# A rotation kernel whose first and last 16 images are cut into four pieces, in 8-row runs

## Chip, cores, metric

One core of one Trainium2 chip. The metric is the device time of one execution in microseconds (us), which in these runs is about 1.8 us more than the span of the profile. All runs compared here are at a granted clock of 1.0. "Tile" below means 16 images (4.2 MB in, 4.2 MB out); there are six, numbered 0 to 5. DVE is the Vector engine; SP and ACT are the engines whose queues issue the loads and the outputs.

## The reference

```python
batch, c, h, w = 32, 3, 256, 256
x = np.random.randn(batch, c, h, w).astype(np.float32)
return np.rot90(x, k=1, axes=(-2, -1)).astype(np.float32)
```

96 images of 256x256 float32 are rotated by 90 degrees: 25.17 MB are read and 25.17 MB written, and nothing is computed.

## The kernel before

A partition holds a run of R = 16 rows of an image, and 32 partitions hold the runs of two images. DVE transposes 32x32 blocks with strided access patterns, so that a partition ends up with 16 rows of the rotated image.

```python
R = 16; K = H // R; A = 32 // K; G = 4 * A * A; F = R * W   # K 16, A 2, G 16, F 4096
x_v = x.rearrange("b c h w -> (b c h w)").rearrange(
    "(g b a qk f) -> g b qk a f", b=A, a=A, qk=4 * K, f=F)
o_v = ...                                                   # [cut: the same for the output, with a and b exchanged]
in_pool = ...tile_pool(name="in_pool", bufs=3)
out_pool = ...tile_pool(name="out_pool", bufs=3)
for g in range(N // G):
    S = in_pool.tile([P, A, F], fp32, name="S")
    for b in range(A):
        nc.sync.dma_start(out=S[:, b], in_=x_v[g, b])       # 2 MB, in 16 KB packets
    U = out_pool.tile([P, A, F], fp32, name="U")
    ...                                                     # [cut: the views src and dst]
    for q in range(R):
        nc.vector.transpose(dst[:, q], src[:, q])           # 16 of 128x512
    for a in range(A):
        nc.scalar.dma_start(out=o_v[g, a], in_=U[:, a])     # 2 MB, in 16 KB packets
```

## Time and profile before

| | before |
|---|---|
| time, median (range) | 124.6 us (124.37 to 124.67) |
| span of the profile | 122.7 us |
| DVE busy | 90.7 us (74%) |
| first DMA packet starts, last one ends | 2.13 us, 121.59 us |
| 16 KB packets per DMA engine, usual duration | 192, 611 ns: 117.3 us |

The first three rows are from the page and the times; the last two are counted from the packet records of the trace. From the page, with the span in 40 slices of 3.07 us (busy tenths for DVE and DMA, then the rate), then the costliest group and the DMA issues:

```profile
span 122.7 us, 182 instructions
DVE 90.7 (74%) x96; POOL 0.2 (0%) x4
...
DVE  0000699999999999999999999999906999930000
...
DMA  3999999999999999999999999999999999999992
GB/s 85 406 433 443 427 427 427 427 427 427 310 432 432 433 433 427 427 433 432 419 433 438 427 427 427 432 438 432 432 427 438 438 427 433 433 427 427 427 432 101
...
L49 DVE STREAM_TRANSPOSE U<-S 128x512 f32<-128x512 f32 x96 | 90.7, 1055 | 17.7 <-DMA S<-in_x_dram 13.3
...
S<-in_x_dram SPq DMA_DIRECT2D x12, 2048.0 KB, 22.3
out_dram<-U ACTq DMA_DIRECT2D x12, 2048.0 KB, 23.3
```

Only one row is full from end to end: DMA. One slice, 31 to 34 us, falls to 310 GB/s; call it the dip. DVE is idle for four slices at the start and four at the end, but DMA is full in nearly all of them.

What DVE waits for (total us, times, longest; a wait of 0.2 us for itself is left out):

```profile
DVE U L49 <- DMA S<-in_x_dram: 13.3, 1, 13.3
DVE U L49 <- DMA out_dram<-U: 4.1, 1, 4.1
```

And the timeline (start us, duration us, engine, line) of the first issue, and of the last tile's transposes:

```profile
0.73 0.60 SPq L43 DMA_DIRECT2D S<-in_x_dram  x1
...
93.14 15.20 DVE L49 STREAM_TRANSPOSE U<-S 128x512 f32<-128x512 f32 x16 [4.15 <-DMA out_dram<-U]
```

The last tile's transposes end at 108.3 us. They are 15.2 us for 16, so 0.95 us from start to start, 1.86 ns per element. The Trainium skill ("Vector Engine (DVE) Microarchitecture Reference", "5.2 Measured stream behaviour on trn2") gives 1.71 to 1.98 ns per column for two-source streams that hop 4 KiB at every element of the output or of all operands, against 1.05 for contiguous ones. The transposes here read and write with strides at every element and lie within that. But they have one source and other steps, and that table has no row for a transpose, so this is a comparison and not an explanation.

### The profile page before, as it was taken

What the parts mean: (1) busy time and instruction counts of PE and PEld (TensorE: products, weight loads), DVE (VectorE), ACT (ScalarE), POOL (GpSimd) and SP (SyncE); (2) the same over time, 40 slices, a digit from 0 to 9 for tenths busy, and PEclk for the clock granted to TensorE, in tenths of its full rate; (3) what the DMA queues carried; (4) which work ended last, traced back from release to release, by engine and by line L of the source; (5) the groups of instructions that cost most, each with busy time, mean ns of one, the idle gap of its engine ahead of it and who ended that gap; (6) DMA issues with size and microseconds to landing.
All of it is one profiled execution on the core that took longest, in us unless ns stands there. A gap on an engine that the chain in (4) does not pass through costs nothing.

```text
span 122.7 us, 182 instructions
## 1 busy us (share of the span) xinstructions
DVE 90.7 (74%) x96; POOL 0.2 (0%) x4
## 2 busy tenths in 40 slices
DVE  0000699999999999999999999999906999930000
POOL 0000000000000000000000000000000000000000
DMA  3999999999999999999999999999999999999992
GB/s 85 406 433 443 427 427 427 427 427 427 310 432 432 433 433 427 427 433 432 419 433 438 427 427 427 432 438 432 432 427 438 438 427 433 433 427 427 427 432 101
DMA packets 3457, 50.34 MB, mean 410 GB/s; under 512 B 384, under 2 KB 384, under 8 KB 384
## 3 DMA queue, kind: packets, MB, share of 16 engines
q1 hardware_dynamic: 1728, 25.17, 48.9%
q10 hardware_dynamic: 1728, 25.17, 47.9%
q14 instruction: 1, 0.01, 0.0%
HBM read 25.17 MB, written 25.17 MB: 410 GB/s over the span
## 4 chain that ended last, share of the span: by engine, by line
DMA 53%; DVE 31%; SPq 1%; issue 1%; DVEq 1%; ACTq 0%
DVE U L49 31%; DMA out_dram<-U 28%; DMA S<-in_x_dram 26%; SPq L43 1%; DVEq L77 1%; ACTq L51 0%; DVEq L49 0%
## 5 line engine op out<-in xcount | busy, mean ns | idle before, releaser
L49 DVE STREAM_TRANSPOSE U<-S 128x512 f32<-128x512 f32 x96 | 90.7, 1055 | 17.7 <-DMA S<-in_x_dram 13.3
L66 POOL MEMSET const-uint8-127<- 128x1 uint8 x1 | 0.1, 102 | 0.0
L66 POOL MEMSET const-bfloat16-1.0<- 128x1 bf16 x1 | 0.1, 101 | 0.0
L66 POOL MEMSET const-float32-0.0<- 128x1 f32 x1 | 0.1, 98 | 0.2 <-issue 0.2
L66 POOL MEMSET const-float32-1.0<- 128x1 f32 x1 | 0.1, 98 | 0.0
## 6 DMA issues: line engine op xcount, KB each, us to landing
S<-in_x_dram SPq DMA_DIRECT2D x12, 2048.0 KB, 22.3
out_dram<-U ACTq DMA_DIRECT2D x12, 2048.0 KB, 23.3
```

Of the source, the lines that this page charges most:

```text
L43: nc.sync.dma_start(out=S[:, b], in_=x_v[g, b])
L49: nc.vector.transpose(dst[:, q], src[:, q])
L66: nc = _bacc.Bacc("TRN2", target_bir_lowering=False, num_devices=1)
L77: with _tile.TileContext(nc) as tc:
```

## The change

The two visible faults of the profile are the 13.3 us before DVE starts and the long end after DVE stops. The change cuts the first and the last tile into four pieces of 4 images: each is loaded, transposed (one 128x2048 instruction with 8-row runs) and put out on its own, so work should start after a quarter of a tile and the last output should be small. The middle four tiles stay as they were. In `KINDS`, 1 is a tile in pieces and 2 is a tile as before.

```diff
+    G = 16
+    KINDS = [1, 2, 2, 2, 2, 1]
+    for g, kind in enumerate(KINDS):
+        S = in_pool.tile([P, F], fp32, name="S")
+        U = out_pool.tile([P, F], fp32, name="U")
+        if kind == 1:
+            R = 8
+            ...                       [cut: views Sv, Uv, xv, ov in 4 contiguous pieces]
+            for s in range(4):
+                nc.sync.dma_start(out=Sv[:, s], in_=xv[s])        # 1 MB, 8 KB packets
+            for s in range(4):
+                src = Sv[:, s].rearrange("p (r k q) -> p q r k", r=R, q=R)[:, ::-1, :, ::-1]
+                dst = Uv[:, s].rearrange("p (q k r) -> p q r k", q=R, r=R)
+                nc.vector.transpose(dst, src)                     # one of 128x2048
+                nc.scalar.dma_start(out=ov[s], in_=Uv[:, s])
+        else:
+            ...                       [cut: R = 16, as before]
```

More of the change, by code (lines that the diff above doesn't have):

```diff
@@ L20 @@
     P = 128
-    R = 16
-    K = H // R
-    A = 32 // K
-    G = 4 * A * A
-    F = R * W
-    fp32 = mybir.dt.float32
-    x_v = x.rearrange("b c h w -> (b c h w)").rearrange(
-        "(g b a qk f) -> g b qk a f", b=A, a=A, qk=4 * K, f=F
-    )
-    o_v = out.rearrange("b c h w -> (b c h w)").rearrange(
-        "(g b a qk f) -> g a qk b f", b=A, a=A, qk=4 * K, f=F
-    )
+    G = 16
+    KINDS = [1, 2, 2, 2, 2, 1]
+    assert len(KINDS) * G == N
+    F = G * H * W // P
+    fp32 = mybir.dt.float32
@@ L37 @@
+    xf = x.rearrange("b c h w -> (b c h w)").rearrange("(g f) -> g f", g=N // G)
+    of = out.rearrange("b c h w -> (b c h w)").rearrange("(g f) -> g f", g=N // G)
     in_pool = ctx.enter_context(tc.tile_pool(name="in_pool", bufs=3))
     out_pool = ctx.enter_context(tc.tile_pool(name="out_pool", bufs=3))
-    for g in range(N // G):
-        S = in_pool.tile([P, A, F], fp32, name="S")
-        for b in range(A):
-            nc.sync.dma_start(out=S[:, b], in_=x_v[g, b])
-        U = out_pool.tile([P, A, F], fp32, name="U")
-        src = S.rearrange("p b (r k q) -> p q r k b", r=R, q=R)[:, ::-1, :, ::-1]
-        dst = U.rearrange("p a (q k r) -> p q r k a", q=R, r=R)
-        for q in range(R):
-            nc.vector.transpose(dst[:, q], src[:, q])
-        for a in range(A):
-            nc.scalar.dma_start(out=o_v[g, a], in_=U[:, a])
+    for g, kind in enumerate(KINDS):
[3 more added lines that the diff above has]
+            R = 8
+            Sv = S.rearrange("p (s f) -> p s f", s=4)
+            Uv = U.rearrange("p (s f) -> p s f", s=4)
+            xv = xf[g].rearrange("(s p f) -> s p f", s=4, p=P)
+            ov = of[g].rearrange("(s p f) -> s p f", s=4, p=P)
+            for s in range(4):
[6 more added lines that the diff above has]
+        else:
+            R = 16
+            Sv = S.rearrange("p (b f) -> p b f", b=2)
+            Uv = U.rearrange("p (a f) -> p a f", a=2)
+            xv = xf[g].rearrange("(b a qk f) -> b qk a f", b=2, a=2, f=F // 2)
+            ov = of[g].rearrange("(b a qk f) -> a qk b f", b=2, a=2, f=F // 2)
+            for b in range(2):
+                nc.sync.dma_start(out=Sv[:, b], in_=xv[b])
+            src = Sv.rearrange("p b (r k q) -> p q r k b", r=R, q=R)[:, ::-1, :, ::-1]
+            dst = Uv.rearrange("p a (q k r) -> p q r k a", q=R, r=R)
+            for q in range(R):
+                nc.vector.transpose(dst[:, q], src[:, q])
+            for a in range(2):
+                nc.scalar.dma_start(out=ov[a], in_=Uv[:, a])
```

## The prediction

> **What bounds it now.** The DMA engines. The page's slices show DMA at 9 or more tenths from about 3 to 120 us of the 122.7 us span, at 427 to 433 GB/s; the Vector engine (DVE) is busy 90.7 us (74%). The packet records of the trace give 611 ns for nearly every 16 KB packet. Moving 2 x 25.17 MB takes each of 16 engines 192 packets, 117.3 us. First packet at 2.13 us, last ends at 121.6 us. Outside the floor are: 2.1 us before the first packet, about 0.4 us of slow first packets, a dip at 31 to 34 us (310 GB/s in that slice, when the outputs' queue starts; about 0.9 us lost), 0.9 us of engines finishing unevenly, 1.1 us of end. The Trainium skill ("DMA: Bandwidth & Descriptors", "Where 436 GB/s comes from") states a ceiling of 435 GB/s; this trace's 429 is 99% of it.
>
> The 13.3 us that the DVE waits at the start cost nothing: input streams at full rate. At the other end the waits view shows the last tile's transposes starting at 93.1 us, after 4.1 us of waiting for tile 2's output, and ending at 108.3 us while a backlog of outputs keeps the DMA full.
>
> **What the change does.**
> - Bytes: unchanged. A third (4 pieces x 2 tiles x 2 directions, 1 MB each) go in 8 KB packets, 128 per engine. Half of 611 ns is 305.5; the one 8 KB packet that ran under load (an instruction fetch) took 309 ns. Cost 128 x 3.5 ns = +0.45 us, an estimate. The same page's "Why small descriptors are slow (HBM only)" gives about 3 cycles per packet, which agrees.
> - DVE: 32 transposes of 128x512 (0.95 us start to start) become 8 of 128x2048. At the same 1.85 ns per element each takes 3.8 us (I allow 2.2 to 4.5), 30 us for 30 us. DVE stays near 90 us.
> - First transpose near 5.7 to 6 us in place of 13.3, first output issued near 10 us in place of 28.6. But these outputs take turns with inputs on a full DMA. Gain on the critical path: none, except that the dip may go or move (0 to -0.9 us).
> - The end: the DMA is full until the end in both; smaller last outputs gain nothing.
> - New semaphore waits for issues: one input of tile 2 waits for the first output, two pieces of the last tile for outputs of tiles 1 and 2. Working out the schedule with packets taking turns, I get no idle DMA for 8-row transposes of up to about 6 us. Beyond 7 us each the last tile becomes DVE-bound (+6 us).
>
> **Prediction.** 124.6 + 0.45 (packets) - 0.5 (half the dip, a guess) = 124.5 us, range 123.3 to 126.0. Faster by over 2%: 3%; within 2%: 93%; slower by over 2%: 4%.
>
> **What would show it right.** DMA slices at 9 from 3 us to the end; 425 to 433 GB/s; first DVE start at 5.5 to 6.5 us with no gain in span; DVE busy 85 to 97 us, a 128x2048 at 3.3 to 4.3 us; a chain made mostly of DMA.
>
> **What would make it wrong.** 8 KB packets clearly slower than 309 ns (each 10 ns more is +1.3 us); 128x2048 transposes above 6 us; slices with DMA under 9 in the middle because a wait for an output holds up inputs; a mix of reads and writes from 10 us on that runs below 427 GB/s, which before's mixed stretch (33 to 93 us) does not show.

## The result, and the profile after

| | before | after |
|---|---|---|
| time, median (range) | 124.56 us (124.37 to 124.67), 4 runs | 124.09 us (124.01 to 124.19), 4 runs |
| ratio | | 0.9965, 95% interval 0.9947 to 0.9982 |
| span | 122.7 us | 122.2 us |
| DVE busy | 90.7 us | 91.3 us |
| first DVE start | 13.33 us | 5.67 us |
| first output issued | 28.58 us | 9.67 us |
| last load's last packet ends | 91.8 us | 105.8 us |
| last transpose ends | 108.3 us | 110.8 us |

A ratio in this document is the mean time of one kernel's fast runs over that of the other's in the same rounds, so it is not quite the ratio of the medians. The time fell by 0.35%, clear of noise and far under 2%. From the page of the changed kernel:

```profile
span 122.2 us, 170 instructions
DVE 91.3 (75%) x72; POOL 0.2 (0%) x4
...
DVE  0199999007999999999999990799999999092000
...
DMA  3999999999999999999999999999999999999993
GB/s 86 424 421 416 375 432 429 426 410 442 418 440 437 437 434 418 429 434 429 429 429 429 434 429 421 453 410 413 464 413 429 445 416 426 442 429 408 429 429 161
...
L65 DVE STREAM_TRANSPOSE U<-S 128x512 f32<-128x512 f32 x64 | 60.5, 1059 | 10.8 <-DMA S<-in_x_dram 7.1
L49 DVE STREAM_TRANSPOSE U<-S 128x2048 f32<-128x2048 f32 x8 | 31.0, 3937 | 8.7 <-DMA S<-in_x_dram 8.7
...
S<-in_x_dram SPq DMA_DIRECT2D x8, 2048.0 KB, 21.1
out_dram<-U ACTq DMA_DIRECT2D x8, 2048.0 KB, 19.0
S<-in_x_dram SPq DMA_DIRECT2D x8, 1024.0 KB, 16.6
out_dram<-U ACTq DMA_DIRECT2D x8, 1024.0 KB, 16.1
```

DVE starts eight microseconds sooner, and then has new holes: at 21 to 28 us, at 73 to 77 us and at 104 to 107 us. DMA is as full as before. The dip is now in the fifth slice (375 GB/s), just ahead of the first output packet, as it was before. The waits and the timeline of the changed kernel:

```profile
DVE U L49 <- DMA S<-in_x_dram: 8.7, 2, 5.7
DVE U L65 <- DMA S<-in_x_dram: 7.1, 1, 7.1
DVE U L65 <- issue: 3.7, 1, 3.7
```

```profile
0.73 0.37 SPq L44 DMA_DIRECT2D S<-in_x_dram  x1
...
92.23 11.57 DVE L49 STREAM_TRANSPOSE U<-S 128x2048 f32<-128x2048 f32 x3
106.87 3.97 DVE L49 STREAM_TRANSPOSE U<-S 128x2048 f32<-128x2048 f32 x1 [3.07 <-DMA S<-in_x_dram]
```

The single wait of 13.3 us at the start has become waits of 5.7, 7.1 and 3.1 us for loads, and one of 3.7 us whose releaser the profile does not show. By the packet records that one, too, was most likely for a load: tile 4's ended at 76.0 us, 1.1 us before its transposes began, while the output that had to leave its buffer was done at 67.1 us. The loads come later because they now share the DMA with outputs from 13.8 us on. Counted from the packets that end between 16 and 26 us, loads moved 282 GB/s and outputs 144 GB/s; before, loads had 421 GB/s there and outputs nothing. That is two to one, which is what the Trainium skill ("DMA: Bandwidth & Descriptors", "Queues, rings and completion order") leads one to expect: an engine takes turns between queues packet by packet, and here a 16 KB packet of a load alternates with an 8 KB packet of an output. Between 60 and 80 us in before, with 16 KB on both sides, the shares are 215 and 217.

The bookkeeping of the DMA, from the packet records of one profile each, in us per engine. "Stretched" is the time by which packets took longer than the usual one of their size; "idle" is engine time without a packet between the first and the last; "overlap" is time with more than 16 packets on record at once.

| | before | after | difference |
|---|---|---|---|
| until the first packet | 2.13 | 1.75 | -0.38 |
| packets at their usual time (611 ns; 309 ns) | 117.31 | 117.76 | +0.45 |
| stretched | 1.27 | 1.23 | -0.04 |
| idle | 1.55 | 1.12 | -0.43 |
| overlap (subtracted) | -0.67 | -0.80 | -0.13 |
| after the last packet | 1.15 | 1.17 | +0.02 |
| span | 122.74 | 122.23 | -0.51 |

The 8 KB packet takes 309 ns, as predicted, and the 128x2048 transpose 3.94 us (3.8 predicted). The term that the prediction does not have is the first: the first packet comes 0.38 us sooner. Most of the idle row is in the last 3 us (0.92 to 0.57 us), where the engines finish unevenly; the experiments below show that this moves between 0.45 and 0.98 us from kernel to kernel where the same 2 MB outputs come last and no gap precedes them, so one profile's difference there proves nothing.

### The profile page after: what moved, and what is told of

It reads as the page before. It is cut to its first block, busy times and chain, and to the rows that moved or that the text cites. A ratio compares the mean times of both kernels' runs of the same rounds, so it can differ in the third digit from the quotient of the medians.

```text
span 122.2 us, 170 instructions
## 1 busy us (share of the span) xinstructions
DVE 91.3 (75%) x72; POOL 0.2 (0%) x4
## 4 chain that ended last, share of the span: by engine, by line
DMA 61%; DVE 27%; issue 1%; SPq 1%
DMA S<-in_x_dram 46%; DVE U L65 24%; DMA out_dram<-U 16%; DVE U L49 3%; SPq L44 1%
## 5 line engine op out<-in xcount | busy, mean ns | idle before, releaser
L65 DVE STREAM_TRANSPOSE U<-S 128x512 f32<-128x512 f32 x64 | 60.5, 1059 | 10.8 <-DMA S<-in_x_dram 7.1
L49 DVE STREAM_TRANSPOSE U<-S 128x2048 f32<-128x2048 f32 x8 | 31.0, 3937 | 8.7 <-DMA S<-in_x_dram 8.7
```

Source lines behind the costliest of these rows:

```text
L49: nc.vector.transpose(dst, src)
```

## The experiments

**Theory.** The DMA is full from the first packet to the last, so time can only change where the DMA starts, in what packets cost, or where a gap opens. **Rivals.** (1) The gain comes from transposes and outputs that start earlier. (2) The finer pieces overlap better by themselves. (3) For the small effects: the first packet is early because the load is small.

### One half of the change at a time

First tile only in pieces:

```diff
-    KINDS = [1, 2, 2, 2, 2, 1]
+    KINDS = [1, 2, 2, 2, 2, 2]
```

> Only the first tile in four pieces. Theory (the DMA is always full, so only the first packet's start, the packets' own time and the unevenness of the last packets count): first packet at 1.75 us as in the changed kernel (-0.38 against before), packets +0.22 us, uneven end 0.9 us as before: time 124.3, 0.1 to 0.4 us below before. Rival (the gain comes from transposes and outputs that start earlier): the whole gain of 0.5 us or more is here. First transpose at 5.7 us in both.

Measured: 126.78 us (126.07 to 126.81), ratio 1.0159 (1.0136 to 1.0183). Both were wrong: the half that starts DVE at 5.6 us costs 2 us. Its page (of the fastest of its five runs, 126.07 us) and the last piece of its timeline:

```profile
DVE  0199997009999999999999952999960999990000
...
DMA  3999999999999999999999999999999999957993
GB/s 90 422 424 430 374 430 443 424 422 432 427 446 424 422 432 411 422 432 427 432 443 438 432 432 422 422 430 427 438 443 432 427 432 422 427 216 327 432 422 169
```

```profile
96.53 15.20 DVE L65 STREAM_TRANSPOSE U<-S 128x512 f32<-128x512 f32 x16 [4.38 <-DMA S<-in_x_dram]
```

There is a hole in the DMA row, in the 36th and 37th of the 40 slices (216 and 327 GB/s). Early outputs took turns from the loads, so the last load's packets end at 95.3 us (91.8 in before) and the last tile's transposes start at 96.5 us (93.1 in before). They take 15.2 us and nothing of that tile can go out until they end at 111.7 us. The outputs queued from earlier tiles run out between 110.2 and 111.1 us, on one DMA engine after the other, and the last tile's first packets start at 113.0 us: 2.46 us of idle DMA for each engine on average, by the packet records. Not all of it is lost: after the gap the engines finish together, with 0.10 us of idle time in the last 3 us in place of 0.92. I had not worked this out for the half change.

Last tile only in pieces:

```diff
-    KINDS = [1, 2, 2, 2, 2, 1]
+    KINDS = [2, 2, 2, 2, 2, 1]
```

> Only the last tile in four pieces. Theory: first packet at 2.13 us as before, packets +0.22 us, idle time of the DMA engines in the last 3 us falls from 0.92 to about 0.57 us: time 124.4, 0 to 0.3 us below before. Rival (an earlier start of the transposes makes the gain): no gain at all, 124.5 to 124.8.

Measured: 124.96 us (124.58 to 125.08), ratio 1.0029 (1.0014 to 1.0044). The theory expected 124.4, so it missed here by 0.5 us, and rival (1) expected 124.5 to 124.8, nearer. The idle time of the last 3 us is 0.57 us as expected, but the profiled run was the fastest of the six (124.58) and its packets were stretched by 0.3 us more than in before. Why the others take 125.0 is open.

So the halves do not add: +2.2 us (first tile alone) and +0.4 us (last tile alone), both by the medians, make -0.5 us together. The pieces at the end repair what the early start breaks: with them only the last quarter of a tile, one transpose of 4 us, stands between the last load and its output.

### Is it the late last load that makes the gap?

Two experiments take the gap away from the half change in two different ways. The first makes the last tile's DVE work short (wrong result):

```diff
 (on e1_first)
-            for q in range(R):
-                nc.vector.transpose(dst[:, q], src[:, q])
+            if g == len(KINDS) - 1:
+                nc.vector.tensor_copy(U, S)
+            else:
+                for q in range(R):
+                    nc.vector.transpose(dst[:, q], src[:, q])
```

> Wrong result on purpose: e1_first (only the first tile in pieces, 126.8 us) with a plain copy in place of the last tile's 16 transposes, about 4.4 us of DVE in place of 15.2. Theory (e1_first is slow because its last load lands 3.4 us later, so that the queued outputs run out at 110.2 us, before the last tile's 15.2 us of transposes are done): the gap of 2.5 us at 110 to 113 us goes, 124.0 to 124.6 us. Rival (8 KB and 16 KB packets together, or the early mix of reads and writes, cost the time): stays above 126.

Measured: 123.98 us, ratio 0.9950 (0.9937 to 0.9963). The copy took 4.43 us, the last load's packets ended as late as ever (95.5 us), and no gap is left.

The second leaves the last tile alone and holds back the first tile's outputs, by a tiny copy from the second tile into them (four elements of each partition wrong; the check of the results let so few pass):

```diff
 (on e1_first)
-                nc.scalar.dma_start(out=ov[s], in_=Uv[:, s])     # first tile
+                held.append((ov[s], Uv[:, s], Uv[:, :, 0]))
 ...
                 nc.vector.transpose(dst[:, q], src[:, q])        # second tile
+                if held and q == 1:
+                    nc.vector.tensor_copy(held[0][2], Uv[:, 0, 256:260])
+                    for o, u, _ in held:
+                        nc.scalar.dma_start(out=o, in_=u)
+                    held = []
```

> e1_first with the first tile's four outputs held back until two transposes of the second tile are done (about 24 to 26 us in place of 9.6 to 21.5 us); four columns of the first tile are wrong on purpose, to make the hold. Same loads, same packets, same transposes otherwise. Theory (early outputs take turns from the loads, so the last load lands late): the last load lands near 87 us in place of 96.5, no gap at 110 us, 124.0 to 124.7 us. Rival (8-row pieces in the first tile are slow in themselves, or 16-row tiles after them): stays above 126.

Measured: 123.92 us (123.83 to 124.06), ratio 0.9949 (0.9936 to 0.9962). From its timeline, the outputs of the first tile and the last two tiles' transposes:

```profile
25.95 1.88 ACTq L70 DMA_DIRECT2D out_dram<-U  x4
...
77.96 30.22 DVE L66 STREAM_TRANSPOSE U<-S 128x512 f32<-128x512 f32 x32 [4.31 <-DMA out_dram<-U]
```

Outputs start at 26 us in place of 9.6, the last load's packets end at 86.8 us in place of 95.3, DVE ends at 108.2 us, and the 2.5 us gap is gone. Apart from the tiny copy, loads, packets and transposes are the same. **Starting the outputs later made the half change 2 to 3 us faster.** The two runs together show the cause: the gap needs both the late last load and 15.2 us of transposes after it, and goes when either is taken away.

### How much slack had DVE in the kernel before?

Before, its share was 74%. Four of the last tile's 16 transposes are done twice (the result stays right):

```diff
-        for q in range(R):
+        extra = 4 if g == N // G - 1 else 0
+        for q in list(range(R)) + list(range(extra)):
             nc.vector.transpose(dst[:, q], src[:, q])
```

> The kernel before, with 4 of the last tile's 16 transposes done a second time (3.8 us more at the end of the DVE chain). Theory: in before the queued outputs last to about 111.8 us and the last tile's first output packet could come at about 110.4, so DVE has only about 1.4 us of slack there: 2.4 us more, 126.9 us (126.4 to 128.2), with a gap in the DMA near 112 us. Rival (DVE has slack, 74% busy): 124.5.

Measured: 126.00 us (125.91 to 126.35), ratio 1.0122 (1.0104 to 1.0140). Slower as expected, but by less than the 126.4 to 128.2 given, with the gap where it was expected. The same 3 us, from 110 to 113 us, of three kernels. The columns are stretch, its length, busy time and count of DVE, of POOL, granted clock, DMA share, GB/s. First before, then the first tile alone in pieces, then four transposes more:

```profile
110.00:113.00 3.00, 0.00 (x0) 0.00 (x0) 1.00 1.01 431
```

```profile
110.00:113.00 3.00, 1.73 (x2) 0.00 (x0) 1.00 0.18 76
```

```profile
110.00:113.00 3.00, 1.76 (x2) 0.00 (x0) 1.00 0.21 87
```

In before the DMA passes this stretch at full rate. In both others DVE is still at its last two transposes and the DMA moves 76 and 87 GB/s. The same stretch in e9_copylast, e11_hold and the changed kernel, where no gap is left:

```profile
110.00:113.00 3.00, 0.00 (x0) 0.00 (x0) 1.00 1.01 431
110.00:113.00 3.00, 0.00 (x0) 0.00 (x0) 1.00 1.02 437
110.00:113.00 3.00, 0.84 (x1) 0.00 (x0) 1.00 0.97 410
```

The extra transposes ended the DVE chain at 111.8 us, 3.4 us later, and 2.1 us of idle DMA appeared: so the chain had 1.3 us to spare, not the 14 us that one might read from its end at 108.3 us and not the 26% that it idles. The time rose by only 1.45 us because here, too, the engines then finished together (0.10 us of idle time in the last 3 us).

The opposite case, almost no DVE work anywhere (one copy for each tile, wrong result):

```diff
-        for q in range(R):
-            nc.vector.transpose(dst[:, q], src[:, q])
+        nc.vector.tensor_copy(U.rearrange("p a f -> p (a f)"), S.rearrange("p b f -> p (b f)"))
```

> Wrong result on purpose: the kernel before with one plain copy of each tile in place of the 16 transposes, so DVE has about a third or less of its work (90.7 us to 25 to 50 us). Theory: DVE is off the critical path everywhere, outputs only start earlier: 124.5 us, within 0.4 of before. Rival (the DVE chain at the start or the end holds part of the time): 1 us or more below before.

Measured: 124.20 us, ratio 0.9972 (0.9959 to 0.9985). DVE was busy 26.6 us in place of 90.7, and 64 us less of it bought 0.35 us. DVE does not bound the kernel.

And each piece's transpose done twice in the changed kernel, to see whether the prediction's limit for them is real:

```diff
                 nc.vector.transpose(dst, src)
+                nc.vector.transpose(dst, src)
```

> The changed kernel with each 128x2048 transpose done twice (7.8 us for a piece, DVE about 122 us; the result stays right). The schedule of the prediction, packets taking turns, says that the last tile then becomes bound by DVE: 12 to 13 us of idle DMA late in the run, 136.7 us (134 to 139). If the DVE had slack everywhere, as its share of 75% alone suggests: 124 to 127 us.

Measured: 133.90 us (two runs), just under the 134 to 139 that I gave. Its page:

```profile
DVE  0299999999999999999999999999999999999950
...
DMA  3999999999999996899999999999999999970355
```

DVE is now the full row and the DMA row has holes at the middle and at the end, 9.7 us of idle time in all. The limit is real, and the method puts it 3 us too high.

### The packets

All six tiles in pieces:

```diff
-    KINDS = [1, 2, 2, 2, 2, 1]
+    KINDS = [1, 1, 1, 1, 1, 1]
```

> All six tiles in 8-row pieces of 1 MB. Theory: every packet 309 ns, 118.66 us of packets per engine (+1.35 against before, +0.90 against the changed kernel), start and end as in the changed kernel: 125.0 us (124.7 to 125.3), DVE 92 us. Rival (finer pieces overlap better): below 124.1.

Measured: 124.47 us (124.45 to 124.75), ratio 0.9995 (0.9982 to 1.0008). Rival (2) fails, but the time lies under the 124.7 to 125.3 expected: the cost of the packets was put too high. They took 309 ns each as expected, yet the rate between 40 and 110 us (averaged over windows whose ends lie within 2 us of these, since a single one can be off by as much as is looked for) was 427.4 GB/s against 430.9 in before, 0.8% less, which over 117 us is 0.95 us and not 1.35. Part of a packet's record overlaps the next one's (overlap 1.02 us against 0.67), so durations from the records should not simply be added. Set against the changed kernel, by the two ratios to before, twice as many additional 8 KB packets cost 0.30% or 0.37 us; the third that the change makes small then costs about 0.2 us by the time and 0.3 us (a third of 0.95) by the rate, both estimates.

### Why does the first packet come 0.38 us sooner?

Three first loads that differ from that of before: in size, in the source's pattern, and in the pattern of both sides.

```diff
 (the condition that limits each edit to the first load is cut)
 (e5_split: two loads of 1 MB, packets of 8 KB, rows in the same pattern)
+                for h in range(2):
+                    c = slice(h * F // 2, (h + 1) * F // 2)
+                    nc.sync.dma_start(out=S[:, b, c], in_=x_v[g, b, :, :, c])
 (e8_contig: two loads of 64 partitions, each a contiguous run, into every second partition)
+                Sa = S.rearrange("(qk a) b f -> a qk b f", a=A)
+                for a in range(A):
+                    nc.sync.dma_start(out=Sa[a, :, b], in_=x_v[g, b, :, a])
 (e12_run: one load of 2 MB, one contiguous run into 128 partitions; wrong on purpose)
+                src_b = x.rearrange("b c h w -> (b c h w)")[: P * F].rearrange("(p f) -> p f", f=F)
```

> The kernel before, with only its very first load (2 MB) cut by columns into two of 1 MB, 8 KB for each packet; the pattern of rows stays as it was. It asks what brings the first packet from 2.13 to 1.75 us. If it is the size (1 MB in 8 KB packets): first packet near 1.75 us and the time 0.2 to 0.4 us below before (packets cost only +0.06). If it is the pattern (one contiguous run in the changed kernel, rows interleaved from two places in before): first packet stays at 2.1 us and the time within 0.2 of before.

> The kernel before, with only its first 2 MB load cut into two loads of 64 partitions each, every one a single contiguous run of the input; packets stay 16 KB and the result right. If the contiguous pattern brings the first packet forward (the split by columns, which kept the interleaved rows, left it at 2.10 us): first packet at 1.6 to 1.9 us and the time 0.2 to 0.4 us below before, 124.2. If not: 2.1 us and 124.5.

> Wrong result on purpose: the kernel before, with its first 2 MB load taken as one contiguous run into 128 partitions (the pattern of the changed kernel's pieces, but 2 MB in 16 KB packets). Its issue took 603 ns in before, 374 ns in the changed kernel, 602 ns where only the size was cut (e5_split) and 544 ns where only the source was contiguous but the tile was written in every second partition (e8_contig). If the pattern of both sides sets it: issue 370 to 400 ns, first packet 1.7 to 1.8 us, time 124.2 (0.2 to 0.5 below before). If the size of the packets must be small as well: 600 ns, 2.1 us, 124.5.

| first load | issue took | first packet | time | ratio (interval) |
|---|---|---|---|---|
| before: 2 MB, interleaved rows | 603 ns | 2.13 us | | |
| after: 1 MB, contiguous | 374 ns | 1.75 us | 124.09 us | 0.9965 (0.9947 to 0.9982) |
| e5_split: 1 MB, interleaved | 602 ns | 2.10 us | 124.29 us | 0.9980 (0.9963 to 0.9997) |
| e8_contig: 1 MB, contiguous, every second partition | 544 ns | 2.05 us | 124.32 us | 0.9986 (0.9966 to 1.0007) |
| e12_run: 2 MB, contiguous | 377 ns | 1.77 us | 124.18 us | 0.9971 (0.9957 to 0.9984) |

The issue that ends it, in the timeline of e12_run:

```profile
0.73 0.38 SPq L46 DMA_DIRECT2D S<-in_x_dram  x1
```

Rival (3) falls: a small load with the old pattern is as late as before, and a big one with the plain pattern as early as after. What brings the first packet forward is a load that is one contiguous run over all 128 partitions; its issue is 0.23 us shorter and its first packet 0.36 us earlier. A contiguous source alone was not enough: e8_contig missed its 1.6 to 1.9 us. e12_run leaves all transposes and outputs of before as they are and gains 0.3%, about as much as the whole change. That the earlier packet makes this gain is likely but not shown: e5_split, expected within 0.2 us of before, was 0.28 us faster by the medians with its first packet as late as before.

### The dip

```diff
-            nc.sync.dma_start(out=S[:, b], in_=x_v[g, b])
+            eng = nc.scalar if g == 0 and b == 1 else nc.sync
+            eng.dma_start(out=S[:, b], in_=x_v[g, b])
```

> The kernel before, with the second half of its first tile loaded from the ACT queue. It asks what the dip at 31 to 34 us is (0.68 us of stretched input packets, no output packet before 33.35 us). If it is the cold start of the ACT queue: the dip goes, up to 0.7 us below before. If it is the first writes that mix with reads, or something else that comes with the outputs: the dip stays near 31 us with 0.5 to 0.8 us of stretched packets and the time is within 0.3 of before.

Measured: 124.68 us, ratio 1.0012 (0.9999 to 1.0026). The ACT queue, whose load was issued at 0.73 us, moved its first packet at 5.0 us, and the dip stayed at 30 to 37 us with 1.1 us of stretched packets. So it is not the first use of that queue. Over the runs it stands at the first output packet, mostly just ahead of it: 31 to 34 us (first output packet at 33.4 us) in before, 11 to 14 us (13.8) in after, 20 to 23 us (22.9) in e4_copy, 28 to 33 us (29.5) in e11_hold. It moves with the first outputs and does not go away; by what mechanism it slows the loads is open.

## Why the prediction was right, and where it was not

- **Bound by the DMA, so the early start gains nothing: right.** 64 us less DVE work gained 0.35 us, and holding the outputs back cost nothing.
- **The time: right.** 124.09 us measured, 124.5 predicted, inside 123.3 to 126.0 and within 2%. That the middle came within half a microsecond is in part luck: the packets were put too dear and the dip's gain too high, two errors of 0.15 to 0.3 us that cancel, and the first packet was left out. The sum said almost no change (-0.05 us); -0.44 was measured.
- **Packets +0.45 us: the 309 ns is right, the sum too large.** e3_all8 puts it at 0.2 to 0.3 us; the records overlap.
- **Dip -0.5 us ("half the dip, a guess"): wrong.** The dip moved with the first outputs and lost little (packets stretched by 0.68 us at 30 to 34 us before, 0.50 us at 10 to 14 us after).
- **Left out: the first packet, -0.38 us.** I read 2.1 us before the first packet as fixed. The load's pattern sets 0.36 us of it, shown by e12_run. With packets at +0.2 to +0.3 us this makes about -0.1 to -0.2 of the measured -0.44 us (0.35% of 124.6), if an earlier first packet saves its time in full; the rest is not settled. The uneven end of the engines, 0.35 us less in the profile of after, could be it, but it varies by more than that among kernels with the same 2 MB outputs last.
- **"The DMA is full until the end in both; smaller last outputs gain nothing": the first part right, the second wrong as a reason.** The DMA is full in both only because the last tile came in pieces together with the early start. With the early start alone there is a gap of 2.5 us. The small pieces gained nothing over before, and saved 2 to 3 us within the change.
- **"I get no idle DMA" up to 6 us for a transpose: consistent, not tested at 6.** At 7.8 us 9.7 us were idle.

No version that was run with a right result beats both kernels clearly: e11_hold (0.9949) and e9_copylast (0.9950) are 0.15% below the changed kernel's ratio with overlapping intervals, and their results are wrong.

## What to carry to other kernels

In these runs, where the DMA is full from the first to the last packet, an output that starts earlier only takes turns from a load that then comes later, and the load that counts is the last one: between its landing and the first packet of its output there must be enough other outputs queued to cover the work on that tile. Compute that cover (here 1.3 us of slack) in place of the engine's idle share before changing either end; here the early start paid only together with a shorter end, or with the first outputs held back. If the first load can be one contiguous run over all partitions, try that alone first; here the run that did so (with a wrong result) was 0.3% faster, though e5_split shows that not all of that need be its doing.

## What the Trainium skill lacked or had wrong

- "DMA: Bandwidth & Descriptors", "Latency and other measured facts", gives about 600 ns to the first byte of a hardware-generated DMA. Here it was 1.40 us from the start of the issue (0.80 us from its end) for a load with interleaved rows, and 1.02 us (0.65 us from its end) for one contiguous run over 128 partitions. The page does not say from which moment it counts. That the pattern sets the issue time, 603 against 374 ns, is on none of the pages that I read.
- The same page, "Why small descriptors are slow (HBM only)", gives about 3 cycles for each packet as a cost. With its 32 bytes per cycle an 8 KB packet is 256 + 3 cycles, so by the 309 ns of the trace 3 cycles are 3.6 ns (an estimate from both). The records put an added packet at 7 ns (two of 309 against one of 611), the rate of e3_all8 at about 5 ns (0.95 us for 192 more packets on each engine) and its time at about 3 ns (0.37 us for 128 more than in after), estimates too. So the records do not agree with the page, and the cost in time comes nearer to it. The prediction compared the 3 cycles with its 3.5 ns, the excess of an 8 KB packet over half of a 16 KB one, which is half the cost of an added packet.
- No page that I read has the time from a queue's first issue to its first packet while another queue's loads fill the DMA (first output packet 4.2 us after its issue at 9.67 us in after, 4.8 us in before; 4.2 us for the load on the ACT queue in e6_actload; what it waits for is open), nor the dip near the first outputs (0.4 to 1.1 us of stretched load packets in every profile taken).
- "Vector Engine (DVE) Microarchitecture Reference", "5.2 Measured stream behaviour on trn2", has the cost of hopping streams but no transpose, and none of the pages searched has a measured time for one with strided float32 patterns ("VectorE: DVE Perf Modes" has one for a plain bf16 block): 1.86 ns per element for 128x512 here, and 3.94 us for a 128x2048.
